# A streaming encoder step on one core: the relative bias copied to DRAM in eight parts, RWKV's low-rank weights loaded in the indexer, and RWKV's output transposed two chunks at a time

## The chip, the core and the metric

One core of a Trainium2 chip runs the whole program. The metric is the device time of one execution in microseconds; the lower, the better. The kernel before was run three times: 1328.97, 1330.21 and 1335.14 us, with a median of 1330.21 us.

## What is computed

One layer of a streaming encoder over 1024 prompt rows and 64 sample rows, with three mixers side by side and one output projection:

```
u = rms_norm(h)                       # 1088 rows x 1024
z = u @ w_in                          # all columns of all branches
A: RWKV-7: per head a 64x64 state, S = S * w + (S . -kk) (kk * a) + v k
   decay from tanh(w_in) @ w_b, rate from a_in @ a_b      (both of rank 64)
   y = group_norm(y) * lnx_w + lnx_b + (r.k.r_k) v
B: forgetting attention, causal, with a cumulated forget gate
C: sparse attention: indexer scores, top 256 keys per row, softmax with
   bias = t5_table[t5_bucket(key position - query position)]
h = h + concat(A * silu, B * silu, C * silu) @ w_out
y = rms_norm(h)
```

The change touches three things of this: how the bias of C comes to DRAM, when the two low-rank matrices `a_w_b` and `a_a_b` of A are loaded, and how the normalised `y` of A is turned to head-major form.

## The kernel before

**Stages.** The input rows are normalised and transposed to `uH` (rounded) and `uL` (the rest). Then the *indexer* projects the columns that the sparse branch's scores need and computes the scores of seven row tiles (`score[2]` to `score[7]` and `score["s"]`). Then *RWKV* works through 17 units of four 64-step chunks, while the top-k search runs beside it on VectorE and ScalarE. Then come the two attentions and the output projection.

**Projections as fill.** Every projection (`proj`, line 154) streams three matmuls per 128 columns of `u`: the weights' bf16 copy `wb` with `uL`, and the split weights `wh` and `wl` with `uH`. The weight tiles come in the order of `PLAN`, one 512 KB tile `wraw` after another (line 130, two buffers); ScalarE rounds it to `wh` (line 137), GpSimd makes `wl` and `wb` from it (lines 140 and 142). Projections of later branches are *fill*: `pump` puts pieces of them between the steps of indexer, RWKV and attention, so that TensorE has work while those wait. A projection writes one of two banks `pproj`; the bank is free when ScalarE and VectorE have read it (lines 802 to 806 in RWKV's inputs: `zs`, `zm`, `shift`).

**Order on the engines.** The program is written as generators that are braided by rates. On top of that, the framework's scheduler orders the instructions of each engine by a simulated timeline; so an instruction runs where its operands are ready by that simulation, and not where its line stands. Each engine works through its queue in order, and all transfers here are issued by SyncE, in order too. A transfer on SyncE that must wait holds up those behind it.

**The bias.** `relative_bias` (line 1242) multiplies the bias table with a one-hot matrix (`t5tab`, `t5oh`, into `t5ps`), copies the 8x384 result to `t5v` in SBUF, and writes it to DRAM 128 times over, as `d_t5` of 128x8x384 (line 1258; `d_t` in the profile). The sparse attention later reads from it a skewed view. The indexer drives this generator in three steps: at row tiles 3, 5 and "s".

**The low-rank weights.** `rwkv_pools` (line 1261) is called when the indexer is done. It loads the two 64x512 matrices twice each into a z tile `wabr` (line 1275), rounds them on ScalarE to `wabh` (line 1276) and leaves the rest in `wabl` on GpSimd (lines 1271 and 1278). `low_rank` (lines 1293 and 1294) multiplies them for every unit.

**The tail of a unit.** `tail` (line 1600) normalises `Yt`, 128 x 4 chunks x 64. Partitions hold two heads, columns a head's 64 values. Each chunk is transposed by itself to 64x128 in `ps_tp` (line 1625, by the helper at line 107), and two activations per span of chunks apply scale and bias (line 1631) from `lnx`, which has 64 partitions.

Of the kernel before, what the change touches and what calls it, by code (L numbers as in the profile page):

```python
# [12 lines left out]
F32 = mybir.dt.float32  # L13
F32R = mybir.dt.float32r
# [3 lines left out]
AF = mybir.ActivationFunctionType  # L18
OP = mybir.AluOpType
# [5 lines left out]
P = 128  # L25
# [60 lines left out]
class K:  # L86
# [183 lines left out]
    def setup(self):  # L270
        nc, I = self.nc, self.I
# [8 lines left out]

        self.trib = cp.tile([P, 2, 512], BF16, name="trib")
        nc.gpsimd.memset(self.trib, 0.0)
        self.lnx = cp.tile([64, 16], F32, name="lnx")
        self.par = cp.tile([P, 54], F32, name="par")
        self.omm = cp.tile([P, 13], F32, name="omm")
        self.par2 = cp.tile([P, 16], F32, name="par2")
# [1 line left out]
        with ExitStack() as c2:  # L288

            xa, xb = [self.xp.tile([P, D], F32, tag=f"x{i}", name="setup", bufs=1) for i in range(2)]  # L290
            rows = xb[:54, 0:P]
            con = xa[:, 0:C_M]
            nc.sync.dma_start(out=con, in_=I["consts"][:, 0:C_M])
            nc.vector.tensor_copy(self.con, con)
            nc.vector.tensor_scalar(self.trib[:, 1, 0:64], con[:, C_AM + 64:C_AM + 128], NEG, None, op0=OP.mult)
            tri = xb[:, P:2 * P]
            nc.sync.dma_start(out=tri, in_=I["consts"][:, C_TRI:C_ALL])
            nc.vector.tensor_copy(self.trib[:, 0, 384:512], tri)
            o = 0
            for nm, n in (("a_mu", 13), ("state_a_shift", 13), ("a_w0", 4), ("a_a0", 4), ("a_k_k", 4), ("a_k_a", 4), ("a_r_k", 4)):  # L300
                src = I[nm]
                names = " ".join(f"x{i}" for i in range(len(src.shape)))
                nc.sync.dma_start(out=rows[o:o + n, :], in_=src.rearrange(f"{names} -> ({names})").rearrange("(a p) -> a p", p=P))
                o += n
            self.PAR = dict(mu=0, sh=13, w0=26, a0=30, kk=34, ka=38, rk=42)
            lrows = xb[:16, 2 * P:2 * P + 64]
            nc.sync.dma_start(out=lrows[0:8, :], in_=I["a_lnx_w"].rearrange("x (a p) -> (x a) p", p=64))
            nc.sync.dma_start(out=lrows[8:16, :], in_=I["a_lnx_b"].rearrange("x (a p) -> (x a) p", p=64))
            ps = self.pt.tile([P, 4, P], F32, tag="xps", name="ps_setup").rearrange("p a b -> p (a b)")
            nc.tensor.transpose(ps[:, :46], rows[:46, :], self.ident[:46, :46])  # L310
            nc.tensor.transpose(ps[:64, 64:80], lrows, self.ident[:16, :16])
            nc.vector.tensor_copy(self.par[:, :46], ps[:, :46])
            nc.vector.tensor_scalar(self.lnx, ps[:64, 64:80], 0.5, None, op0=OP.mult)
        nc.vector.tensor_scalar(self.omm, self.par[:, 0:13], -1.0, 1.0, op0=OP.mult, op1=OP.add)

        nc.vector.tensor_scalar(self.par2[:, 0:4], self.par[:, 26:30], 0.5, None, op0=OP.mult)
# [81 lines left out]
    def indexer(self):  # L398
# [6 lines left out]
        with ExitStack() as c2:  # L405
# [54 lines left out]
            for i in list(range(2, 8)) + ["s"]:  # L460

                if i == 3:
                    gates = self.forget(ip, mrow)
                    next(gates)
                    bias = self.relative_bias(c2)
                    next(bias)
                if i == 4:
                    nc.sync.dma_start(out=O["p_c_kidx"][0, 0].rearrange("(a p) d -> p a d", p=P), in_=mrow[:, 0:8, 0:64])
                    nc.sync.dma_start(out=O["s_c_kidx"][0, 0], in_=mrow[:64, 8, 0:64])
                if i == 5:  # L470
                    next(bias)
                if i == 7:
                    next(gates, None)
                if i == "s":
                    next(bias, None)
                r = P if i != "s" else 64
                q0 = i * P - 256 if i != "s" else 768
                k0, kn = (0, (i + 1) * P) if i != "s" else (1024, 576)
# [763 lines left out]
    def relative_bias(self, ctx):  # L1242

        nc = self.nc
        self.d_t5 = self.dram.tile([P, 8, 384], F32, tag="d_t5", name="d_t5")
        p = self.pool("t5", ctx=ctx, right=True)
        pp = self.pool("t5p", space=PSUM, ctx=ctx, right=True)
        tb = p.tile([32, 8], F32, name="t5tab")
        oh = p.tile([32, 384], F32, name="t5oh")
        nc.sync.dma_start(out=tb, in_=self.I["t5_table"])  # L1250
        nc.sync.dma_start(out=oh, in_=self.I["onehot"])
        yield
        ps = pp.tile([P, 512], F32, name="t5ps")
        nc.tensor.matmul(ps[:8, :384], tb, oh, start=True, stop=True)
        vv = p.tile([8, 384], F32, name="t5v")
        nc.vector.tensor_copy(vv, ps[:8, :384])
        yield
        nc.sync.dma_start(out=self.d_t5.rearrange("q h r -> h q r"), in_=vv.rearrange("h (o r) -> h o r", o=1).broadcast_to([8, P, 384]))


    def rwkv_pools(self, c2):


        nc, I, O = self.nc, self.I, self.O
        one = self.pool("rw1", ctx=c2, right=True)
        self.gen = self.pool("gen", space=PSUM, ctx=c2)
        self.gring = lambda tag, bufs: (lambda dt=F32: self.gen.tile([P, 512], dt, tag=tag, name="ps_" + tag, bufs=bufs))

        self.wabh = one.tile([P, 2, 512], F32R, name="wabh")
        self.wabl = one.tile([P, 2, 512], F32R, name="wabl")  # L1270
        nc.gpsimd.memset(self.wabl.bitcast(F32), 0.0)
        raw = self.z("wabr")[:, 0:1024].rearrange("p (x c) -> p x c", x=2)
        for x, nm in enumerate(("a_w_b", "a_a_b")):
            for r in (slice(0, 64), slice(64, 128)):
                nc.sync.dma_start(out=raw[r, x], in_=I[nm][0])
        nc.scalar.copy(self.wabh, raw)
        for x, r in enumerate((slice(0, 64), slice(64, 128))):
            nc.gpsimd.tensor_tensor(self.wabl[r, x], raw[r, x], self.wabh[r, x], op=OP.subtract)
        self.one, self.state = one, None

        self.ND = [one.tile([P, 2, 4, P], F16, name=f"ND{i}") for i in range(2)]
        for t in self.ND:
            nc.gpsimd.memset(t, 0.0)
# [316 lines left out]
    def tail(self, one, x):  # L1600
# [20 lines left out]
        (g if PN & 2 else v).tensor_tensor(Yt, Yt, bc(st[:, 2]), op=OP.mult)  # L1621
        yield
        ps = self.tp()
        for c in range(4):
            self.turn(ps[0:64, c * P:c * P + P], Yt[:, c])
        q = ps[0:64].rearrange("p (c x t) -> p c x t", x=2, t=64)
        for hp, t0, o, n in x["spans"]:
            cs = slice(o // 64, (o + n) // 64)
            for h in range(2):
                hd = 2 * hp + h  # L1630
                sc.activation(yT[hv[h], cs], q[:, cs, 1 - h], AF.Identity, bias=self.lnx[:, 8 + hd:9 + hd], scale=self.lnx[:, hd:hd + 1])
        y = yT.rearrange("p c t -> p (c t)")
        g.tensor_tensor(y, y, x["vb"].rearrange("p c t -> p (c t)"), op=OP.add)
        g.tensor_tensor(y, y, gt, op=OP.mult)
# [121 lines left out]
def program(ctx, tc, I, O):  # L1756
# [24 lines left out]
    s.setup()  # L1781
    cx.close()
    with ExitStack() as c2:
        s.zs = s.pool("zs", bufs=1, ctx=c2, right=True)
        s.scp = s.pool("scp", ctx=c2, right=True)
        s.tkp = s.pool("tkp", ctx=c2, right=True)
# [19 lines left out]
        for u in range(n + 2):  # L1806
# [12 lines left out]
            if u < n:  # L1819
                work.append(("topk", topk, N_TOPK, (DVE, ACT)))  # L1820
            work = [w[:3] for w in work if w[0] != "topk"]
            s.free = u >= FE
            s.braid(work, R_T if u > n else R_END if len(work) < 3 and u else R_A / 10, ("topk", topk, N_TOPK, (DVE, ACT), work[-1][0] if SIDE < 0 else work[SIDE][0]) if u < n else None)
        for _ in topk:
# [89 lines left out]
```

## Time and profile before

| | |
|---|---|
| median of three runs | 1330.21 us |
| the profiled execution | 1331.56 us |
| its span | 1329.8 us |
| mean granted clock of TensorE | 0.979 |
| TensorE busy | 1258.4 us |
| VectorE, ScalarE, GpSimd busy | 847.5, 780.2, 669.7 us |
| moved by transfers | 168.78 MB, mean 127 GB/s |

In the profile PE is TensorE, PEld its weight loads, DVE VectorE, ACT ScalarE, POOL GpSimd and SP SyncE. An arrow `a<-b` reads: a written from b. What stands in brackets at the end of a row of the timeline is how long the engine stood before it, and what ended that. PEclk is the granted clock: 1.00 is 2.4 GHz, 0.50 is 1.2 GHz.

### The profile page before, as it was taken

How to read it: one execution, taken by the hardware profiler on the slowest of the kernel's cores; microseconds unless marked ns; L12 is line 12 of the kernel's file. 1: busy time of each engine (PE TensorE's matmuls, PEld its weight loads, DVE VectorE, ACT ScalarE, POOL GpSimd, SP SyncE). 2: the span in 40 equal slices, each digit the busy share in tenths (PEclk: the TensorE clock that was granted, in tenths of full speed). 3: DMA queues.
4: the chain of work that ended last, by engine and by line, in shares of the span. 5: the costliest groups of instructions: out<-in, count | busy, mean ns of one | idle time of the engine just before them, and what ended most of it. 6: DMA issues, size and time to landing. Idle time of an engine off the chain costs nothing.

```text
span 1329.8 us, 29357 instructions
## 1 busy us (share of the span) xinstructions
PE 1258.4 (95%) x10544; PEld 964.2 (73%) x10563; DVE 847.5 (64%) x2487; ACT 780.2 (59%) x1762; POOL 669.7 (50%) x973
## 2 busy tenths in 40 slices
PE   7969999999999999988999998999999989999997
PEld 5747676777777777766777677888988856777764
DVE  7338437887877777899754316556666479766642
ACT  7335427777777887644353346576665578655532
POOL 6223445445445456556464365566667567544311
PEclk9979999999999999988999998999999989999999
DMA  7352422222223324433232378867755576543323
GB/s 224 50 105 71 128 83 66 87 70 89 68 70 104 102 80 140 123 101 110 94 104 89 126 216 246 217 201 209 182 198 146 146 212 186 142 116 106 97 76 95
DMA packets 172460, 168.78 MB, mean 127 GB/s; under 512 B 38513, under 2 KB 147097, under 8 KB 172314
## 3 DMA queue, kind: packets, MB, share of 16 engines
q1 hardware_dynamic: 172314, 166.89, 43.9%
q8 instruction: 84, 1.38, 0.4%
q14 instruction: 62, 0.51, 0.1%
HBM read 104.61 MB, written 62.24 MB: 125 GB/s over the span
## 4 chain that ended last, share of the span: by engine, by line
PE 73%; DVE 11%; DMA 6%; ACT 3%; issue 3%; POOL 2%; SPq 1%; DVEq 0%; POOLq 0%; ACTq 0%
PE pproj L154 32%; PE pproj L1697 7%; PE ps_pv L993 5%; PE ps_atp L107 5%; PE ps_tp L1697 4%; PE ps_ga L1412 3%; DMA wraw<-in_w_in_dram 2%; PE ps_sc L962 2%; PE ps_sc L963 2%; PE ps_gb L1471 2%; PE ps_tp L107 1%; PE ps_gb L1478 1%; PE ps_gc L1581 1%; ACT junka L601 1%; PE ps_gc L1583 1%
## 5 line engine op out<-in xcount | busy, mean ns | idle before, releaser
L154 PE MATMUL pproj<-uH,wh 128*128 128x384 f32 (+4 forms) x1088 | 494.6, 455 | 0.0
L154 PE MATMUL pproj<-uH,wl 128*128 128x384 f32 (+4 forms) x1088 | 363.4, 334 | 0.0
L154 PE MATMUL pproj<-uL,wb 128*128 128x384 bf16 (+4 forms) x1088 | 359.4, 330 | 2.2 <-DVE shift L806 2.0
L154 PEld LDWEIGHTS pproj<-uH,wh 128*128 128x128 f32 (+1 forms) x1088 | 217.9, 200 | 3.9 <-issue 0.7
L154 PEld LDWEIGHTS pproj<-uH,wl 128*128 128x128 f32 (+1 forms) x1088 | 208.1, 191 | 2.2 <-issue 0.2
L154 PEld LDWEIGHTS <-wb 128*128 128x128 bf16 (+1 forms) x1088 | 106.6, 98 | 118.6 <-issue 81.5
L601 ACT ACTIVATE junka<-score,tk_tau 128x1024 f16<-128x1024 f32 (+4 forms) x160 | 149.4, 934 | 38.9 <-DVE junk L595 24.1
L914 POOL TENSOR_SCALAR S<-S,mx 128x128 f32<-128x128 f32 (+8 forms) x136 | 103.8, 766 | 83.7 <-DVE mx L913 60.4
L931 ACT CAST hl<-ps_atp 128x512 fp32r<-128x512 f32 (+3 forms) x184 | 93.4, 514 | 77.7 <-PE ps_atp L107 68.2
L140 POOL TENSOR_TENSOR wl<-wraw,wh 128x256 fp32r<-128x256 f32 (+1 forms) x184 | 137.1, 775 | 3.3 <-ACT wh L137 2.7
L932 DVE TENSOR_TENSOR hl<-ps_atp,hl 128x512 fp32r<-128x512 f32 (+3 forms) x184 | 109.7, 600 | 44.6 <-ACT hl L931 42.8
L142 POOL TENSOR_SCALAR wb<-wraw 128x512 bf16<-128x512 f32 (+1 forms) x92 | 60.3, 671 | 142.1 <-issue 60.7
L909 ACT ACTIVATE S<-S,mx 128x128 f32<-128x128 f32 (+8 forms) x136 | 105.8, 778 | 38.2 <-DVE mx L905 34.8
L993 PE MATMUL ps_pv<-hl,VS 128*128 128x256 f32 (+3 forms) x640 | 113.7, 290 | 7.7 <-ACT hl L931 3.2
L993 PEld LDWEIGHTS ps_pv<-hl,VS 128*128 128x128 f32 (+1 forms) x640 | 90.4, 176 | 20.8 <-DVE hl L932 5.0
L107 PE MATMUL ps_atp<-ident,S 128*128 128x128 f32 x616 | 103.6, 280 | 1.1 <-POOL S L914 0.8
L1159 POOL TENSOR_TENSOR cb<-nm,T 128x256 f32<-128x256 bf16 (+2 forms) x80 | 57.4, 724 | 52.7 <-DVE mx L905 51.1
L107 PEld LDWEIGHTS ps_atp<-ident,S 128*128 128x128 f32 x616 | 76.4, 144 | 7.7 <-issue 1.7
L137 ACT CAST wh<-wraw 128x1024 fp32r<-128x1024 f32 (+1 forms) x46 | 47.7, 1038 | 47.0 <-PE pproj L154 27.0
L1697 PE MATMUL pproj<-oh,gh 128*128 128x512 f32 x144 | 67.4, 490 | 0.6 <-ACT pproj L1745 0.3
L803 DVE SCALAR_TENSOR_TENSOR zm<-pproj,omm,zs 128x384 f32<-128x384 f32 (+2 forms) x52 | 25.8, 496 | 43.3 <-ACT zs L802 42.9
L1697 PE MATMUL pproj<-ol,gb 128*128 128x512 bf16 (+1 forms) x134 | 48.8, 386 | 1.4 <-DVE ol L1677 0.9
(383 smaller groups left out, 2849.6 us busy)
## 6 DMA issues: line engine op xcount, KB each, us to landing
wraw<-in_w_in_dram SPq DMA_DIRECT2D x45, 512.0 KB
oraw<-in_w_out_dram SPq DMA_DIRECT2D x12, 512.0 KB
out_dram<-rows SPq DMA_DIRECT2D x10, 512.0 KB
x<-in_x_prompt_dram SPq DMA_DIRECT2D x8, 512.0 KB
wt<-a_wa SPq DMA_DIRECT2D x16, 256.0 KB
b_v<-vs SPq DMA_DIRECT2D x8, 512.0 KB
VS<-b_v SPq DMA_DIRECT2D x8, 512.0 KB
d_y<-y SPq DMA_DIRECT2D x64, 64.0 KB
```

Of the source, the lines that this page charges most:

```text
L107: self.nc.tensor.transpose(out, x, self.ident[:n, :n])
L140: nc.gpsimd.tensor_tensor(l[:, k:k + 2, :n], raw[:, k:k + 2, :n], h[:, k:k + 2, :n], op=OP.subtract)
L142: nc.gpsimd.tensor_scalar(b[:, k:k + 4, :n], raw[:, k:k + 4, :n], 1.0, 0.0, op0=OP.mult, op1=OP.add)
L154: self.nc.tensor.matmul(ps[:n, :nt], a[:, k, :n], b[:, k, t0:t0 + nt], start=(k == 0 and i == 0), stop=(k == KD - 1 and i == 2))
L601: nc.scalar.activation(junk[:, :sc.shape[1]], sc, AF.Sign, bias=tf[:, j:j + 1], accum_out=cnt[:, j:j + 1])
L909: nc.scalar.activation(S[:, :kn], S[:, :kn], AF.Exp, bias=mx[:, nm - 1:nm], scale=-1.0, accum_out=mx[:, 6:7])
L914: nc.gpsimd.tensor_scalar(S[:, :kn], S[:, :kn], mx[:, 7:8], 0.5, op0=OP.mult, op1=OP.mult)
L931: nc.scalar.copy(ph[:kr, a:b], ps[:kr, a:b])
L932: nc.vector.tensor_tensor(pl[:kr, a:b], ps[:kr, a:b], ph[:kr, a:b], op=OP.subtract)
L993: nc.tensor.matmul(pv[0:m, q0:256], VS[:, kb, 0:m], hl[:, x, o:o + w], start=kb == 0 and x == 0, stop=at[-1][0] == last and n == 3)
L1159: nc.gpsimd.tensor_tensor(o, x, y, op=OP.add)
L1697: nc.tensor.matmul(ps[hf][:n, :], parts[m // 4][q][:, m % 4, :n], self.wo[m][q // 2][:, hf * 512:hf * 512 + 512], start=m == 0 and q == 0, ...
```

## The change

Three parts. The bias goes from `t5v` to one row `d_row` of 8x384 in DRAM, and from there in eight transfers of 16 copies each to `d_t5`; the generator yields between them, one step per RWKV unit from the second on. The loads and the splitting of the low-rank weights move into the indexer, at row tiles 3 and 5; the raw weights stay in the memory of `score[7]` until that tile's scores are written, and `wabh` and `wabl` have a pool of their own. In the tail, two chunks are transposed at once, 128x128, so that odd chunks come out on partitions 64 to 127; `lnx` gets a second copy on those partitions, and a span of several chunks takes four activations instead of two.

```diff
-        self.lnx = cp.tile([64, 16], F32, name="lnx")
+        self.lnx = cp.tile([P, 16], F32, name="lnx")
...
-            lrows = xb[:16, 2 * P:2 * P + 64]
-            nc.sync.dma_start(out=lrows[0:8, :], in_=I["a_lnx_w"].rearrange("x (a p) -> (x a) p", p=64))
-            nc.sync.dma_start(out=lrows[8:16, :], in_=I["a_lnx_b"].rearrange("x (a p) -> (x a) p", p=64))
+            lrows = xb[:16, 2 * P:3 * P]
+            for c in (slice(0, 64), slice(64, P)):
+                nc.sync.dma_start(out=lrows[0:8, c], in_=I["a_lnx_w"].rearrange("x (a p) -> (x a) p", p=64))
+                nc.sync.dma_start(out=lrows[8:16, c], in_=I["a_lnx_b"].rearrange("x (a p) -> (x a) p", p=64))
...
                 if i == 3:
...
-                    bias = self.relative_bias(c2)
-                    next(bias)
+                    self.bias = self.relative_bias(c2)
+                    next(self.bias)
+                    self.load_low_rank()
...
                 if i == 5:
-                    next(bias)
+                    next(self.bias)
+                    self.split_low_rank()
...
                 if i == "s":
-                    next(bias, None)
+                    next(self.bias)
...
         yield
-        nc.sync.dma_start(out=self.d_t5.rearrange("q h r -> h q r"), in_=vv.rearrange("h (o r) -> h o r", o=1).broadcast_to([8, P, 384]))
+        nc.sync.dma_start(out=row[:, :], in_=vv)
+        yield
+        for q in range(0, P, 16):
+            nc.sync.dma_start(out=self.d_t5[q:q + 16], in_=row.rearrange("(o h) r -> o h r", o=1).broadcast_to([16, 8, 384]))
+            yield
+
+    def load_low_rank(self):
+        nc, p = self.nc, self.lr
+        self.wabh = p.tile([P, 2, 512], F32R, name="wabh")
+        self.wabl = p.tile([P, 2, 512], F32R, name="wabl")
+        nc.gpsimd.memset(self.wabl.bitcast(F32), 0.0)
+        self.wabr = self.score[7].rearrange("p (x c) -> p x c", x=2)
+        for x, nm in enumerate(("a_w_b", "a_a_b")):
+            for r in (slice(0, 64), slice(64, 128)):
+                nc.sync.dma_start(out=self.wabr[r, x], in_=self.I[nm][0])
+
+    def split_low_rank(self):
+        nc = self.nc
+        nc.scalar.copy(self.wabh, self.wabr)
+        for x, r in enumerate((slice(0, 64), slice(64, 128))):
+            nc.gpsimd.tensor_tensor(self.wabl[r, x], self.wabr[r, x], self.wabh[r, x], op=OP.subtract)
...
-        for c in range(4):
-            self.turn(ps[0:64, c * P:c * P + P], Yt[:, c])
-        q = ps[0:64].rearrange("p (c x t) -> p c x t", x=2, t=64)
+        for j in range(2):
+            self.turn(ps[:, j * P:j * P + P], Yt[:, 2 * j:2 * j + 2].rearrange("p c t -> p (c t)"))
+        q = ps[:, :256].rearrange("p (j x t) -> p j x t", x=2, t=64)
         for hp, t0, o, n in x["spans"]:
-            cs = slice(o // 64, (o + n) // 64)
+            c0, c1 = o // 64, (o + n) // 64
             for h in range(2):
                 hd = 2 * hp + h
-                sc.activation(yT[hv[h], cs], q[:, cs, 1 - h], AF.Identity, bias=self.lnx[:, 8 + hd:9 + hd], scale=self.lnx[:, hd:hd + 1])
+                for i in range(2) if c1 - c0 > 1 else (c0 % 2,):
+                    sc.activation(yT[hv[h], (c0 + i if c1 - c0 > 1 else c0):c1:2], q[hv[i], c0 // 2:(c1 + 1) // 2, 1 - h], AF.Identity,
+                                  bias=self.lnx[hv[i], 8 + hd:9 + hd], scale=self.lnx[hv[i], hd:hd + 1])
...
+            if u:
+                next(s.bias, None)
             s.free = u >= FE
```

The six lines of `rwkv_pools` that loaded and split the low-rank weights are gone.

Since the scheduler decides the order, the places are shown as they come out. First SyncE's queue, near the end of the indexer's first projections. Before, `t5tab` and `t5oh` are the table and the one-hot matrix, `d_t_822` is the bias in DRAM and `wraw` a weight tile:

```order
L130 DMA wraw<-in_w_in_dram 128x8x128 x2
L1250 DMA t5tab<-in_t_table_dram 32x8
L1251 DMA t5oh<-in_onehot_dram 32x384
L1258 DMA d_t_822<-t5v 8x128x384
L130 DMA wraw<-in_w_in_dram 128x8x128 x2
L468 DMA out_dram<-mrow 128x8x64
```

And with the change, where `score_418` is the memory of `score[7]`:

```order
L130 DMA wraw<-in_w_in_dram 128x8x128 x2
L1254 DMA t5tab<-in_t_table_dram 32x8
L1255 DMA t5oh<-in_onehot_dram 32x384
L1278 DMA score_418<-in_a_w_b_dram 64x512 x2
L1278 DMA score_418<-in_a_a_b_dram 64x512 x2
L1262 DMA d_row<-t5v 8x384
L1265 DMA d_t_828<-d_row 16x3072 x8
L130 DMA wraw<-in_w_in_dram 128x8x128 x2
L470 DMA out_dram<-mrow 128x8x64
```

The four loads and the copy to `d_row` stand ahead of the bias copy; its eight parts stand together where the one transfer stood, between the same weight loads.

Second, TensorE where the first RWKV unit is prepared beside a projection. Before:

```order
L154 LDWEIGHTS wb
L154 MATMUL pproj<-uL,wb 128x320
L154 MATMUL pproj<-uH,wh 128x320
L154 MATMUL pproj<-uH,wl 128x320
L1293 MATMUL ps_ga<-wt,wabh 128x256
L1294 MATMUL ps_ga<-wt,wabl 128x256
L1331 MATMUL ps_ga<-ones,k_1709 128x2 x2
L154 LDWEIGHTS wb
```

And with the change:

```order
L154 MATMUL pproj<-uH,wl 128x384
L1307 MATMUL ps_ga<-wt,wabh 128x256
L1308 MATMUL ps_ga<-wt,wabl 128x256
L154 LDWEIGHTS wb
L154 MATMUL pproj<-uL,wb 128x320
L154 MATMUL pproj<-uH,wh 128x320
L154 MATMUL pproj<-uH,wl 128x320
```

The two low-rank matmuls stand four groups of 128x320 further ahead, right behind the last group of 128x384; the one with `ones` follows two groups later.

Third, GpSimd in the indexer, with the change; before, `wl` of line 140 is followed by `wb` of line 142 at once:

```order
L140 TENSOR_TENSOR wl<-wraw,wh 128x256 x4
L1274 MEMSET wabl 128x1024
L1284 TENSOR_TENSOR wabl<-score_418,wabh 64x512 x2
L142 TENSOR_SCALAR wb<-wraw 128x512 x2
L140 TENSOR_TENSOR wl<-wraw,wh 128x256 x4
```

The clearing and the two subtractions stand between two weight tiles, of which the second is the one whose `wb` starts at 53.64 us in the profile before. ScalarE's cast to `wabh` stands behind the second `KI` cast of the second key projection.

## Rows read from the trace of the kernel before

**Rows 1.** The page: busy time of the engines, and the chain by engine.

```profile
PE 1258.4 (95%) x10544; PEld 964.2 (73%) x10563; DVE 847.5 (64%) x2487; ACT 780.2 (59%) x1762; POOL 669.7 (50%) x973
...
PE 73%; DVE 11%; DMA 6%; ACT 3%; issue 3%; POOL 2%; SPq 1%; DVEq 0%; POOLq 0%; ACTq 0%
```

**Rows 2.** Timeline of TensorE, 74 to 90 us: start, duration, instruction.

```profile
74.89 0.34 PE L154 MATMUL pproj<-uL,wb 128*128 128x384 bf16 x1
...
75.42 0.34 PE L154 MATMUL pproj<-uL,wb 128*128 128x384 bf16 x1
...
75.77 0.34 PE L154 MATMUL pproj<-uH,wl 128*128 128x384 f32 x1
85.65 0.34 PE L453 MATMUL ps_tp<-ident,mT 76*64 76x76 f32 x1 [9.54 <-ACT mrow L454]
87.98 0.50 PE L154 MATMUL pproj<-uL,wb 128*128 128x384 bf16 x1 [2.00 <-DVE shift L806]
...
88.93 0.54 PE L154 MATMUL pproj<-uL,wb 128*128 128x384 bf16 x1
```

**Rows 3.** The chain that ended last, and ScalarE's timeline, between 57 and 85 us.

```profile
57.80 26.16 DMA wraw<-in_w_in_dram
...
84.06 1.04 ACT L137 CAST wh<-wraw 128x1024 fp32r<-128x1024 f32 x1 [15.09 <-DMA wraw<-in_w_in_dram]
```

**Rows 4.** The chain: a weight tile at 203.60 us, a 64 KB load at 1007.26 us.

```profile
203.60 4.20 DMA wraw<-in_w_in_dram
...
1007.26 2.23 DMA cQ<-c_q1h
```

**Rows 5.** Issues on SyncE between 40 and 50 us; size of the bias copy.

```profile
40.47 0.33 SPq L1251 DMA_DIRECT2D t5oh<-in_onehot_dram  x1
49.62 0.29 SPq L1258 DMA_DIRECT2D d_t<-t5v  x1
...
d_t<-t5v SPq DMA_DIRECT2D x1, 1536.0 KB
```

**Rows 6.** Windows: busy time by engine (PE, PEld, DVE, ACT, POOL), clock, DMA share, GB/s.

```profile
64.00:76.00 12.00, 12.00 (x75) 8.84 (x73) 1.24 (x2) 1.38 (x4) 0.00 (x0) 1.00 0.45 51
...
92.00:94.00 2.00, 2.00 (x11) 1.54 (x10) 0.54 (x3) 0.60 (x1) 2.00 (x4) 0.78 0.70 139
...
154.00:158.00 4.00, 4.00 (x25) 2.89 (x24) 1.59 (x4) 0.58 (x1) 4.00 (x6) 1.00 0.83 271
```

**Rows 7.** Where RWKV begins: timelines of TensorE and ScalarE, and one window.

```profile
164.32 0.38 PE L1293 MATMUL ps_ga<-wt,wabh 128*128 128x256 f32 x1 [2.12 <-ACT wabh L1276]
165.71 0.58 PE L1294 MATMUL ps_ga<-wt,wabl 128*128 128x256 f32 x1 [1.01 <-POOL wabl L1278]
...
158.06 0.51 ACT L1327 ACTIVATE k<-zt,par 128x256 f32<-128x256 f32 x1 [1.22 <-DMA zt<-a_k]
...
163.22 1.04 ACT L1276 CAST wabh<-wabr 128x1024 fp32r<-128x1024 f32 x1 [2.17 <-DMA wabr<-in_a_a_b_dram]
...
164.00:172.00 8.00, 6.68 (x26) 5.22 (x27) 1.77 (x4) 3.15 (x8) 5.98 (x8) 0.57 0.27 76
```

**Rows 8.** RWKV's stage, 160 to 800 us, as one window.

```profile
160.00:800.00 640.00, 612.58 (x6666) 460.18 (x6665) 432.57 (x1330) 392.46 (x912) 334.38 (x512) 0.98 0.34 103
```

**Rows 9.** Timeline of GpSimd, its first weight tile after the normalisation.

```profile
53.64 1.20 POOL L142 TENSOR_SCALAR wb<-wraw 128x512 bf16<-128x512 f32 x2 [21.27 <-PE pproj L154]
```

**Rows 10.** Timeline of TensorE: four transposes of either width, and one that follows.

```profile
262.93 0.60 PE L107 MATMUL ps_tp<-ident,Yt 128*64 128x128 f32 x4
263.46 0.33 PE L1564 MATMUL ps_gd<-za,UD 64*64 64x64 f32 x4
...
181.81 0.60 PE L107 MATMUL ps_ga<-ident,BK 128*128 128x128 f32 x4
```

**Rows 11.** ScalarE's groups by shape, line 1631: busy us, mean ns.

```profile
L1631 ACT ACTIVATE yT<-ps_tp,lnx 64x256 f32<-64x256 f32 x32 | 17.9, 558 | 5.3 <-PE ps_tp L107 4.8
L1631 ACT ACTIVATE yT<-ps_tp,lnx 64x64 f32<-64x64 f32 x8 | 3.2, 400 | 0.1
```

More of the change, by code (lines that the diff above doesn't have):

```diff
@@ L305, in setup @@
             self.PAR = dict(mu=0, sh=13, w0=26, a0=30, kk=34, ka=38, rk=42)
-            lrows = xb[:16, 2 * P:2 * P + 64]
-            nc.sync.dma_start(out=lrows[0:8, :], in_=I["a_lnx_w"].rearrange("x (a p) -> (x a) p", p=64))
-            nc.sync.dma_start(out=lrows[8:16, :], in_=I["a_lnx_b"].rearrange("x (a p) -> (x a) p", p=64))
+            lrows = xb[:16, 2 * P:3 * P]
+            for c in (slice(0, 64), slice(64, P)):
+                nc.sync.dma_start(out=lrows[0:8, c], in_=I["a_lnx_w"].rearrange("x (a p) -> (x a) p", p=64))
+                nc.sync.dma_start(out=lrows[8:16, c], in_=I["a_lnx_b"].rearrange("x (a p) -> (x a) p", p=64))
             ps = self.pt.tile([P, 4, P], F32, tag="xps", name="ps_setup").rearrange("p a b -> p (a b)")
             nc.tensor.transpose(ps[:, :46], rows[:46, :], self.ident[:46, :46])
-            nc.tensor.transpose(ps[:64, 64:80], lrows, self.ident[:16, :16])
+            nc.tensor.transpose(ps[:, 64:80], lrows, self.ident[:16, :16])
             nc.vector.tensor_copy(self.par[:, :46], ps[:, :46])
-            nc.vector.tensor_scalar(self.lnx, ps[:64, 64:80], 0.5, None, op0=OP.mult)
+            nc.vector.tensor_scalar(self.lnx, ps[:, 64:80], 0.5, None, op0=OP.mult)
         nc.vector.tensor_scalar(self.omm, self.par[:, 0:13], -1.0, 1.0, op0=OP.mult, op1=OP.add)
@@ L1244, in relative_bias @@
         nc = self.nc
+        row = self.dram.tile([8, 384], F32, tag="d_row", name="d_row")
         self.d_t5 = self.dram.tile([P, 8, 384], F32, tag="d_t5", name="d_t5")
@@ L1267, in rwkv_pools @@
         self.gring = lambda tag, bufs: (lambda dt=F32: self.gen.tile([P, 512], dt, tag=tag, name="ps_" + tag, bufs=bufs))
[L1269 to L1278, printed above, removed]
         self.one, self.state = one, None
@@ L1783, in program @@
     with ExitStack() as c2:
+        s.lr = s.pool("lr", ctx=c2, right=True)
         s.zs = s.pool("zs", bufs=1, ctx=c2, right=True)
```

## The prediction

> **What bounds the kernel now.** I read the page first: TensorE is busy for 95% of the span, and 73% of the chain that ended last is TensorE work [rows 1]. So the end moves by what TensorE gains or loses, and the 71 us in which it stands are the first thing to look for. In the page's 40 slices I looked for those where TensorE falls below nine tenths, and opened the timeline there. The largest stand runs from the end of the projection matmul of 75.77 us to 87.98 us with a single small transpose in between [rows 2]. The waits name the cause in steps. That transpose waits for ScalarE's copy of mrow; ScalarE, in order, stood in front of `wh` for a weight tile, 15.09 us until 84.06 us [rows 3]. The tile's transfer was issued at 57.80 us and landed 26.16 us later [rows 3], where an undisturbed one takes 4.20 us [rows 4]. What lay in its way is the copy of the relative bias `d_t`, one transfer of 1536 KB issued at 49.62 us [rows 5]: where it runs alone, 0.45 of the 16 DMA engines are busy and 51 GB/s move [rows 6]. 0.45 of 16 is 7 engines, and 1.573 MB at 51 GB/s is 30.8 us; with the weight loads that share those engines it fills the time to that landing.
>
> A second, smaller stand lies where the indexer ends and the first RWKV unit is prepared: TensorE waits 2.12 us for `wabh` and 1.01 us for `wabl`, which waited for the loads of the raw weights, and works at half clock until about 171 us [rows 7]. From there to 800 us TensorE stands for only 27.4 us of 640 [rows 8].
>
> **The bias copy.** The program spreads the eight parts over RWKV's units, but the order on SyncE, printed above, has all eight right behind `d_row`, ahead of the same two weight loads as before. So nothing is spread; what changes is the shape. The source is a 12 KB row in DRAM, the outer size is 16 instead of 8, and a short copy to `d_row` is added, for which SyncE waits. That wait is covered: between the issue at 49.62 us and that at 57.80 us SyncE has nothing else to issue [rows 3, 5]. In numbers: `t5v` is there at 49.6 us [rows 5]; `d_row` lands after some 2.2 us, by a 64 KB load's row [rows 4]; eight issues at 0.29 us, the issue of the old copy, take 2.3 us. The parts move from about 52 us. No row shows a DRAM-to-DRAM copy, so its rate is bounded. At the old pace of an engine, but on 16 of them, it is 51 / 0.45 = 113 GB/s and 13.9 us; at the 271 GB/s of the stretch in which RWKV's first stores and loads run at a share of 0.83 [rows 6], it is 5.8 us. They end at 58 to 66 us. I take the fast end, the row of traffic on all engines. The weight tile, issued at 57.80 us behind them, lands 4.20 us later, at 62 to 70 us.
>
> The Trainium skill, page "DMA: Bandwidth & Descriptors", section "Rules for kernel authors", says that an outermost size below 16 confines a transfer to at most so many engines; the 0.45 agrees with eight or fewer, and by this rule alone the new shape would run on all 16 and rival (a) below would be out. If the rule held and an engine kept its pace, the copy would take the 13.9 us of the slow bound and the sum would stay; if it did not hold, (a) gives the time.
>
> What is late next? Before, 4.0 us pass from the landing (83.96 us) to the free projection bank for which TensorE waits last (87.98 us) [rows 2, 3]. A tile that lands by 72 us is therefore early enough for TensorE at 76.1 us, and both bounds are. So the stand goes whole: 11.9 us less 0.2 for the transpose in it, 11.7. Behind it the granted clock stays at 0.5, the level of 1.2 GHz, until about 92.9 us [rows 6]; at 0.5 a group of three matmuls takes 0.95 us, at full clock 0.53, start to next start [rows 2], so of 4.9 us 2.2 go. **Term 1: -13.9 us.**
>
> **The low-rank weights.** On SyncE their four loads now follow the one-hot table's, whose issue is at 40.47 us, and SyncE's next issue before is at 49.62 us [rows 5]. GpSimd's clearing and subtractions lie in its 21.27 us of standing that end at 53.64 us [rows 9]. If the loads land 4.20 us after the last issue, as a tile does [rows 4], that is near 47 us; ScalarE's cast, 1.04 us [rows 7], would wait for them a microsecond or two and make the bias row late by as much. 2 us move the slow bound of the tile to 72 us and no further, so I cost it at 0; without that slack each microsecond would cost one. At the old place the wait for `wabh`, 2.12 us, and for `wabl`, 1.01 us, go. The clock's mean of 0.57 from 164 to 172 us [rows 7] makes 6.9 us at 0.5; 5.7 of them are work, which would take 3.1 by the groups above, so 2.6 go. The other inputs hold nothing up: `zt` was there for ScalarE at 158.06 us [rows 7], and the `a_wa` rows were issued just ahead of it; the two matmuls, moved up by four groups (`ones` by two), would run from about 160 us. **Term 2: -5.8 us.**
>
> **The turned output.** Per unit four transposes take 0.53 us of TensorE, start to next start, and the row of four is 0.60 long whether the stationary operand is 64 or 128 wide [rows 10]; two take 0.26. 17 units by 0.27 us: **term 3: -4.5 us**, as TensorE bounds that stretch. ScalarE pays: two activations of 64x256 at 558 ns become four of 64x128, between 400 and 558, say 455 [rows 11]: +0.7 us in 16 units, 11 us. ScalarE is busy for 392 of 640 us there, and all of TensorE's waits together are 27.4 us [rows 8]. Bounds are 0 and +11 us; I take 0, as 3% more of an engine with 39% free falls mostly into its own waits. The two further loads of `lnx` (0.29 us each on SyncE) precede weights that GpSimd takes up at 53.64 us only; 0.
>
> **The sum.** The profiled execution took 1331.56 us: -13.9 - 5.8 - 4.5 = -24.2 gives 1307.4. It stands 1.35 us over the median of the runs, 1330.21; against that, **1306 us**. The new sequence of ready times also changes the scheduler's order in all of RWKV's stage (some hundred rows on each engine change places). That I can't work out; I allow 10 us to either side, about a third of what TensorE stands there.
>
> **Rivals.** (a) *The copy is no faster.* All sixteen engines read one 12 KB row; if 51 GB/s is the pace of the source and not of seven engines, the parts run from 52 to 83 us and the tile, now behind them on every engine, lands at 87 us, 3 us later than before: +3 - 5.8 - 4.5 = -7.3, 1323 us. For it: no row shows such a read. Against it: 0.45 looks like a limit of engines.
> (b) *The copy is slower, and the kernel too.* The place is the same stand. The kernel is slower from where the tile lands later than 83.96 + 10.3 = 94.3 us, which is a copy of 38 us or 41 GB/s; by over 0.5% below 35 GB/s. At 25 GB/s, half the old pace, it lands at 119 us: +35 - 10.3, 1355 us. For it: source and destination share DRAM for the first time. Against it: 271 GB/s of stores to and loads from DRAM go side by side [rows 6].
> (c) *The new order gives it back.* RWKV's stage stands half as much again (+13.7: 1320 us) or twice (+27.4: 1333 us), most likely through ScalarE, whose top-k counts and the two further activations now meet differently. For it: VectorE's and ScalarE's rows change places throughout. Against it: term 1 lies before all of that, and the fill work that covers RWKV's waits is the same.
> (d) *Parts spread as written* would free the DMA engines even more, with the same term 1; it gives the same time.
>
> **How the numbers follow.** Forecast, with (d): 0.74, 1296 to 1316 us. (a): 0.09, about half on each side of 0.5%. (b): 0.06. (c): 0.11, half and half. A measurement of this kernel can tell about 0.5%, 6.7 us, from no change; so faster means below 1323.5 us: 0.74 + 0.05 + 0.06 = 0.85, the same 0.09, slower 0.06. The range is 1296 to 1321: the forecast's own, with the near part of (a) and (c).
>
> **What would show it.** Right: in the new profile the eight parts' window is under 15 us long with the DMA share near 1, the tile lands before 72 us, TensorE has no stand over 3 us between 50 and 100 us, the wait for `wabh` is gone, and the first RWKV matmul stands some 16 us earlier. Wrong: a tile that lands after 76 us ((a), (b)), or TensorE's idle time in RWKV's stage well above 27 us (c). If the stand at 76 us is gone and the end has not moved by 20 us, terms 2 and 3 or the new order failed, and the windows by stage tell which.

## The result, and the profile after

The change takes 1323.20 us, the median of 7 runs (1321.18 to 1325.77), against 1330.21 us before: a ratio of 0.9937 with a 95% interval of 0.992 to 0.9954. It is faster by some 7 us, just over the 0.5% that the prediction calls the least that can be told, where 24 were forecast; 1323.2 lies above the range of 1296 to 1321 us. The page after answers to [rows 1]; TensorE is as much the bound as before, and ScalarE is 10.9 us busier:

```profile
PE 1255.2 (95%) x10529; PEld 959.0 (73%) x10529; DVE 844.9 (64%) x2487; ACT 791.1 (60%) x1794; POOL 664.0 (50%) x973
...
PE 72%; DVE 9%; DMA 7%; ACT 4%; issue 3%; POOL 2%; SPq 2%; POOLq 0%; DVEq 0%; ACTq 0%
```

What the forecast said of the first 170 us is there. SyncE's timeline after (start, duration, instruction; answers to [rows 5]) has the short copy, the eight parts and the weight tile behind them:

```profile
48.63 0.29 SPq L1262 DMA_DIRECT2D d_row<-t5v  x1
50.00 4.96 SPq L1265 DMA_DIRECT2D d_t<-d_row  x8
56.79 0.40 SPq L130 DMA_DIRECT2D wraw<-in_w_in_dram  x1
```

Windows after, columns as in [rows 6]: while the parts run, the DMA engines are all busy (share 1.02) and move 289 GB/s. Where TensorE stood before [rows 2], it is busy without a gap, at full clock, and so it is where RWKV begins [rows 7]:

```profile
52.00:56.00 4.00, 4.00 (x23) 2.66 (x21) 1.14 (x2) 2.23 (x4) 3.28 (x5) 1.00 1.02 289
70.00:88.00 18.00, 18.00 (x106) 13.40 (x106) 15.00 (x40) 11.79 (x22) 10.06 (x13) 1.00 0.42 107
155.00:167.00 12.00, 12.00 (x80) 8.88 (x78) 4.65 (x14) 3.62 (x8) 4.66 (x10) 1.00 0.27 76
```

ScalarE's `wh` from the tile of 56.79 us runs at 70.87 us and waits for a projection there, no longer for the transfer:

```profile
70.87 1.05 ACT L137 CAST wh<-wraw 128x1024 fp32r<-128x1024 f32 x1 [2.89 <-PE pproj L154]
```

The loss lies behind. I cut both executions where TensorE first multiplies `QR` with `BK` (line 1412, now 1426) and at the first scores of the forgetting attention: the stages up to RWKV, RWKV, and the rest. Before:

```profile
0.00:186.91 186.91, 163.05 (x912) 120.75 (x912) 102.07 (x238) 86.25 (x171) 71.73 (x101) 0.95 0.44 112
186.91:791.78 604.87, 581.27 (x6486) 436.74 (x6485) 421.12 (x1293) 377.27 (x877) 316.19 (x483) 0.99 0.33 100
791.78:1329.80 538.02, 514.07 (x3148) 406.68 (x3167) 324.31 (x957) 316.67 (x715) 281.78 (x390) 0.98 0.58 163
```

After:

```profile
0.00:165.85 165.85, 157.13 (x910) 116.64 (x911) 102.22 (x237) 85.62 (x171) 72.74 (x101) 0.99 0.44 126
165.85:776.82 610.97, 580.79 (x6454) 435.63 (x6453) 419.56 (x1293) 391.22 (x910) 315.05 (x483) 0.98 0.33 99
776.82:1320.10 543.28, 517.29 (x3167) 406.69 (x3167) 323.10 (x957) 314.23 (x714) 276.18 (x390) 0.97 0.57 161
```

| stage | forecast | measured |
|---|---|---|
| up to RWKV | -13.9 - 5.8 = -19.7 | -21.1 |
| RWKV | -4.5 | +6.1 |
| the rest | 0 | +5.3 |
| span | -24.2 | -9.7 |

In RWKV's stage TensorE stands 611.0 - 580.8 = 30.2 us, before 23.6, and its busy time fell by only 0.5, at a granted clock of 0.98 instead of 0.99. Its longest waits there (what waited, for what: total, times, longest) end in VectorE's writes:

```profile
PE ps_gc L1586 <- DVE UV L1583: 4.6, 5, 2.7
PE ps_gb L1485 <- DVE Y L1523: 3.4, 6, 1.0
PE ps_gc L1595 <- DVE S L1591: 3.3, 6, 1.0
...
PE ps_gb L1485 <- DVE tk_need L659: 1.9, 1, 1.9
```

So did most of them before: summed by engine, VectorE ends 17.7 of the 21.6 us that this view lists for the stage before, and 22.3 of 28.8 after. The growth is spread over several of its writes.

### The profile page after: what moved, and what is told of

It is laid out like the page before. It is cut to its first block, busy times and chain, and to the rows that moved or that the text cites. A ratio compares the mean times of both kernels' runs of the same rounds, so it can differ in the third digit from the quotient of the medians.

```text
span 1320.1 us, 29357 instructions
## 1 busy us (share of the span) xinstructions
PE 1255.2 (95%) x10529; PEld 959.0 (73%) x10529; DVE 844.9 (64%) x2487; ACT 791.1 (60%) x1794; POOL 664.0 (50%) x973
## 4 chain that ended last, share of the span: by engine, by line
PE 72%; DVE 9%; DMA 7%; ACT 4%; issue 3%; POOL 2%; SPq 2%; POOLq 0%; DVEq 0%; ACTq 0%
PE pproj L154 34%; PE pproj L1714 6%; PE ps_pv L996 4%; PE ps_atp L107 4%; PE ps_tp L1714 3%; PE ps_ga L1426 2%; PE ps_sc L965 2%; PE ps_sc L966 2%; PE ps_gb L1485 2%; PE ps_gb L1492 1%; PE ps_gc L1595 1%; ACT junka L604 1%; DMA oraw<-in_w_out_dram 1%; PE ps_gc L1597 1%; PE ps_tp L107 1%
## 5 line engine op out<-in xcount | busy, mean ns | idle before, releaser
L140 POOL TENSOR_TENSOR wl<-wraw,wh 128x256 fp32r<-128x256 f32 (+1 forms) x184 | 134.2, 761 | 3.6 <-ACT wh L137 2.8
L1162 POOL TENSOR_TENSOR cb<-nm,T 128x256 f32<-128x256 bf16 (+2 forms) x80 | 50.5, 637 | 61.1 <-DVE mx L908 42.7
L1714 PE MATMUL pproj<-ol,gb 128*128 128x512 bf16 (+1 forms) x144 | 52.6, 391 | 0.2 <-DVE ol L1694 0.2
L1583 DVE COPY UV<-ps_gd 64x64 f32<-64x64 f32 x136 | 29.9, 220 | 34.9 <-PE ps_gd L1578 32.2
```

Of the source, the lines that this page charges most:

```text
L140: nc.gpsimd.tensor_tensor(l[:, k:k + 2, :n], raw[:, k:k + 2, :n], h[:, k:k + 2, :n], op=OP.subtract)
L1162: nc.gpsimd.tensor_tensor(o, x, y, op=OP.add)
L1714: nc.tensor.matmul(ps[hf][:n, :], parts[m // 4][q][:, m % 4, :n], self.wo[m][q // 2][:, hf * 512:hf * 512 + 512], start=m == 0 and q == 0, ...
```

## The experiments

Three theories. **S**: ScalarE's two further activations per unit make TensorE stand. **O**: the new order does, whatever the instructions. **L**: a lead is lost whatever one does, since later stages run into something fixed. The same cut of each kernel's own windows gives this table; "stands" is the stage less TensorE's busy time in it, from one trace per kernel, all in us. The ratio is to the kernel before on the same chip; since the experiments ran on several chips, kernels are best compared by it. e5 and e11 leave values out of the result. "Order" is explained at e9.

| kernel | RWKV starts | RWKV takes | stands | the rest | median | ratio (95%) |
|---|---|---|---|---|---|---|
| before | 186.9 | 604.9 | 23.6 | 538.0 | 1330.2 | 1 |
| the change | 165.9 | 611.0 | 30.2 | 543.3 | 1323.2 | 0.9937 (0.992-0.9954) |
| e1 bias copy alone | 172.6 | 607.4 | 23.1 | 538.6 | 1319.1 | 0.9906 (0.9881-0.9931) |
| e2 low rank alone | 181.3 | 608.6 | 21.9 | 539.6 | 1331.2 | 0.9998 (0.998-1.0016) |
| e3 tail alone | 189.1 | 608.4 | 30.2 | 537.4 | 1337.4 | 1.004 (1.0022-1.0057) |
| e4 no tail | 168.1 | 603.1 | 23.5 | 538.7 | 1313.4 | 0.987 (0.9845-0.9896) |
| e7 no tail, lnx | 167.7 | 603.2 | 24.0 | 540.4 | 1317.2 | 0.9889 (0.9866-0.9913) |
| e12 no tail, order 64 | 168.1 | 607.9 | 22.4 | 536.5 | 1315.6 | 0.9881 (0.9854-0.9909) |
| e6 four and four | 167.4 | 607.2 | 24.5 | 541.2 | 1318.1 | 0.9897 (0.9877-0.9916) |
| e16 the same, order 60 | 167.8 | 609.2 | 24.1 | 538.3 | 1309.1 | 0.9835 (0.981-0.986) |
| e17 the same, order 63 | 167.8 | 603.7 | 22.9 | 538.0 | 1314.5 | 0.9874 (0.9855-0.9893) |
| e5 two activations | 166.4 | 598.9 | 20.7 | 536.9 | 1304.4 | 0.9798 (0.9777-0.9819) |
| e11 the same, order 62 | 166.4 | 604.7 | 26.7 | 540.1 | 1313.2 | 0.9857 (0.9834-0.988) |
| e8 odd on VectorE | 167.8 | 599.7 | 20.7 | 541.7 | 1311.0 | 0.9842 (0.9819-0.9864) |
| e14 the same, order 63 | 166.5 | 600.6 | 21.0 | 538.0 | 1309.6 | 0.9832 (0.9807-0.9856) |
| e15 the same, order 60 | 166.9 | 604.5 | 25.3 | 538.2 | 1310.1 | 0.9839 (0.9814-0.9863) |
| e9 the change, order 60 | 167.2 | 612.6 | 27.2 | 539.2 | 1323.5 | 0.9931 (0.991-0.9953) |
| e10 the change, order 63 | 166.2 | 613.8 | 32.8 | 538.3 | 1317.8 | 0.9889 (0.9867-0.9911) |
| e18 the change, order 64 | 166.6 | 618.0 | 34.6 | 543.5 | 1329.4 | 0.9977 (0.996-0.9995) |
| e13 eight activations | 166.9 | 615.4 | 33.9 | 539.7 | 1324.9 | 0.9958 (0.9938-0.9977) |

### The parts one by one

e1 to e4 take hunks of the diff as they stand. In e1 the two calls for the low-rank weights are left out of the bias's hunks; e2 has these calls, their two functions and the pool; e3 has the tail's hunks and those of `lnx`; e4 is the change without e3's hunks.

e1, bias copy alone:

> The kernel before with the bias copy of the change alone; the order of every engine is that of before, but for the copy's own rows on SyncE. Theory O (the new order gives back): with the old order nothing is given back, so term 1 alone and in full: -13.9, about 1316 us, RWKV's TensorE idle 23 to 24 us as before. Theory L (a lead is given back, whatever the order, because the stages behind run into something that doesn't move): some 10 us are lost behind 175 us here too, 1325 us or more. Theory S (ScalarE's further activations in the tail give back): as O, 1316 us.

Measured: 0.9906, 12.5 us less, and the order of all other work is that of before. RWKV starts 14.3 us earlier, and 11.2 of them are left at the end of the trace, with 23.1 us of stands in RWKV's stage as before. So L falls: a lead is not lost by itself.

e2, low-rank weights alone:

> The kernel before with the low-rank weights moved alone; the scheduler reorders about as much as in the whole change. Theory O: term 2 (-5.8) is seen at the start of RWKV, and RWKV's and the attentions' stages differ from before by several us in either direction, so anywhere from 1320 to 1335 us, with the difference in stands and half clock behind 190 us. Theory L: about 1326 to 1330, the lead melts. Theory S: the full term 2, 1324 to 1325 us, and stages behind as before within 1 us.

Measured: RWKV starts 5.6 us earlier, as term 2 says, but the kernel is no faster. The stands are not what took it (21.9); TensorE is busy 586.7 us in RWKV's stage instead of 581.3 with the same instructions, at a clock of 0.98 instead of 0.99:

```profile
181.31:789.94 608.63, 586.70 (x6487) 440.31 (x6487) 420.79 (x1293) 378.57 (x878) 316.44 (x483) 0.98 0.33 99
```

S expected the full 5.8 and O anything; no gain is O's outcome, but the stands, by which O would take it back, are S's. Whether the order brings the lower clock or this one execution had it, one trace doesn't tell. Beside the bias copy the same part gave about what it should: from e1 to e4 the ratio falls from 0.9906 to 0.987, 4.8 us, though the two intervals overlap.

e3, tail alone:

> The kernel before with the two transposes and four activations of the tail alone (and the second copy of lnx); reordered too. Theory O: TensorE's work falls by 4 us, stands differ from before by several us in either direction: 1318 to 1335 us. Theory S: slower by 4 to 8 us, 1334 to 1338, with RWKV's TensorE waiting for ScalarE. Theory L: no lead, so term 3 holds: 1326 us.

Measured: slower by 0.4%, 5.3 us, inside S's 4 to 8. L's 1326 is out, and 1337.4 us lies 2 us above O's range. The stands are 30.2 us, the number of the whole change. But they are not the waits that S named: most of them end in VectorE's writes, few in ScalarE's (22.2 and 3.2 of the 26.9 us that the view lists).

e4, the change without its tail:

> The whole change without its tail: bias copy and low-rank weights, order of e2. Theory O: the time of e2 less 13.9 us. Theory S: terms 1 and 2 in full, -19.7, 1310 us. Theory L: as the whole change or slower, 1323 to 1327 us.

Measured: 1313.4 us, a ratio of 0.987: between S's 1310 and O's 1317, and L is out again. It is faster than the whole change by the 0.0067 between the ratios, 9 us, with 23.5 us of stands. The tail, forecast at -4.5 us, costs 9 beside the other two parts.

### What of the tail costs

e5 gives each span of several chunks two activations again (the even chunks' half, read twice):

```diff
-                for i in range(2) if c1 - c0 > 1 else (c0 % 2,):
-                    sc.activation(yT[hv[h], (c0 + i if c1 - c0 > 1 else c0):c1:2], q[hv[i], c0 // 2:(c1 + 1) // 2, 1 - h], AF.Identity,
...
+                    sc.activation(yT[hv[h], cs].rearrange("p (j i) t -> p j i t", i=2), q[hv[0], c0 // 2:c1 // 2, 1 - h].rearrange("p j (i t) -> p j i t", i=1).broadcast_to([64, m, 2, 64]), AF.Identity,
```

> The whole change, but a span of several chunks takes two activations of 64x256 again, as before: they read the even chunks' half of the turned tile twice, so the odd chunks' values are left out of the result. Two transposes stay, ScalarE's further 11 us go. Theory S (the two further activations of a unit make TensorE stand): RWKV's stage stands 23 to 24 us, as in e1, e2 and e4, and not 30 as in e3 and the whole change; e4's time less term 3, about 1309 us. Theory O (the tail's new order, whatever its activations): 30 us of stands or another number, time anywhere from 1309 to 1325. Theory W (it is the wide transposes that come late or hold TensorE): 30 us, about 1323.

Measured: 1304.4 us with 20.7 us of stands, both a little below what S said; W is out, and the time is below O's range too. RWKV's stage takes 12.1 us less than with four activations:

```profile
166.37:765.27 598.90, 578.20 (x6453) 433.38 (x6453) 417.28 (x1293) 379.74 (x878) 317.38 (x483) 0.99 0.33 101
```

e6 is the other half: e4 with `for i in range(2)` and every second chunk per activation, from four transposes:

> The change without its wide transposes: e4 with each span's two activations split into four of 64x128, from four transposes as before. ScalarE's further 11 us come alone. Theory S: RWKV's stands rise from 23.5 (e4) to about 30 us, with e4's time of 1313.4 plus 7 to 9, 1320 to 1322 us. Theory W: as e4, 1313 us. Theory O: stands between 22 and 32, 1311 to 1322 us, no rule.

Measured: 24.5 us of stands, as W said and not the 30 of S; 1318.1 us lies between the two, by the ratio 3.6 us above e4 and 1 above e7, within the intervals. O's wide range holds it as well. RWKV's window:

```profile
167.40:774.60 607.20, 582.72 (x6487) 438.20 (x6487) 420.10 (x1293) 386.11 (x910) 313.85 (x483) 0.99 0.33 100
```

ScalarE's timelines show the instructions, the two of before, e6's four and the change's four, each row one span:

```profile
263.57 1.13 ACT L1631 ACTIVATE yT<-ps_tp,lnx 64x256 f32<-64x256 f32 x2 [2.45 <-PE ps_tp L107]
```

```profile
243.04 1.61 ACT L1646 ACTIVATE yT<-ps_tp,lnx 64x128 f32<-64x128 f32 x4 [1.01 <-PE ps_tp L107]
```

```profile
241.27 1.86 ACT L1647 ACTIVATE yT<-ps_tp,lnx 64x128 f32<-64x128 f32 x4 [0.80 <-PE ps_tp L107]
```

e7 is e4 with the second copy of `lnx`, which nothing reads:

> e4 with the second copy of lnx alone: two further small loads at the start, nothing else added. The scheduler moves some hundred rows on each engine. It measures what a change of order without a change of work does. Theories S and W: as e4, 1312 to 1315 us, RWKV's stands 22 to 25 us. Theory O: stands move by 3 us or more, time by as much.

Measured: RWKV's stage as in e4 to 0.1 us, with 24.0 us of stands, as S and W said; the rest 1.7 us longer. The median of 1317.2 us is above their 1315, but by the ratio it is 2.5 us from e4, within the intervals. This small change of order was worth next to nothing in RWKV's stage.

e8 keeps the two wide transposes and gives the odd chunks to VectorE:

```diff
+                    elif ENG == "v" and i:
+                        v.tensor_scalar(dst, src, s_, b_, op0=OP.mult, op1=OP.add)
+                    else:
+                        sc.activation(dst, src, AF.Identity, bias=b_, scale=s_)
...
+ENG = "v"
```

> The whole change, with the odd chunks' scale and bias on VectorE, the even ones' on ScalarE. ScalarE is 3 to 4 us less busy than before, VectorE some 10 more. Theory S: the stands go back to about 24 us if it is ScalarE's time that counts, 1309 to 1313 us; if VectorE is as short of time, they stay at 30, 1320 us. Theory W: 1323 us. Theory O: between.

Measured: 1311.0 us, as S said for the case that it is ScalarE's time, with 20.7 us of stands where it said about 24; W is out. VectorE is 428.5 us busy in RWKV's stage, 9 more than in the change, and the stands don't show it:

```profile
167.80:767.50 599.70, 578.99 (x6454) 433.40 (x6453) 428.53 (x1329) 373.19 (x874) 314.45 (x483) 0.99 0.33 101
```

### Other orders of the same instructions

The scheduler's simulated timeline takes 61 cycles for a ScalarE read from PSUM. Set to another number, it gives another order of instructions that are otherwise the same:

```diff
+    _spec.ACCESS_CYCLES = {**_spec.ACCESS_CYCLES, (_b.MemoryType.PSUM, mybir.EngineType.Activation): 60}
```

e9 and e10, the whole change with 60 and 63:

> The whole change, every instruction the same; only the number of cycles that the scheduler's simulated timeline takes for a ScalarE read from PSUM is 60 instead of 61, so the order comes out anew. Theory S (ScalarE's two further activations make TensorE stand, in whatever order): RWKV's stage again stands near 30 us and takes 608 to 612 us, 1320 to 1326 us in all. Theory O (it was this order, and the activations only drew it): the stands fall anywhere between 20 and 30 us, and the time between 1304 and 1326, most likely under 1318.

> As e9 with 63 cycles: another order of the same instructions. Theory S: near 30 us of stands, 1320 to 1326 us. Theory O: not both of e9 and e10 near 30 us; at least one under 1318 us.

Measured: stands of 27.2 and 32.8 us, RWKV's stage 612.6 and 613.8. So the loss in RWKV is not this one order's. The times divide: e9's 1323.5 us is S's, e10's 1317.8 is below S's 1320 and just under O's 1318. The rest of the program, behind RWKV, takes 539.2 and 538.3 us instead of 543.3, with 21.3 and 22.1 us of stands instead of 26.0: so the change's 5.3 us there come with its own order or its one execution, not with its instructions; over all kernels of the table the rest takes 536.5 to 543.5 us.

e11 is e5 with 62, e12 is e4 with 64:

> As e5 (two activations, the odd chunks' values left out) with 62 cycles in the scheduler's timeline: another order of the same instructions. Theory S: as e5, 1302 to 1308 us, 19 to 23 us of stands. Theory O: 1304 to 1326, as likely above 1310 as below.

> As e4 (the change without its tail) with 64 cycles: another order of the same instructions. Theory S: as e4 and e7, 1312 to 1318 us, 22 to 25 us of stands. Theory O: 1306 to 1326 us, and a difference to e4 of 4 us or more either way.

Measured: e11 1313.2 us, above S's 1302 to 1308, with 26.7 us of stands; e12 1315.6 us with 22.4, as S said. Order alone moves RWKV's stage by up to 6 us (e5 to e11). In the stands the groups still don't overlap, if only by 0.5 us (26.7 against e9's 27.2).

### Load, and its company

e13 runs over `(0, 1, 0, 1)`, every activation twice; e14 and e15 are e8 with 63 and 60:

> The whole change with each span's four activations done twice; the result is the same, ScalarE is busy some 29 us more. So far RWKV's stage takes 599 to 605 us with two of them on ScalarE (e5, e8, e11) and 611 to 614 with four (the change, e9, e10), about one us for each us of ScalarE. Theory S: it grows on, to 625 to 645 us, and the time to 1336 to 1355 us. Theory O (the order, not ScalarE's load): 605 to 615 us again, 1315 to 1327 us.

> e8 with 63 cycles in the scheduler's timeline: another order of the same instructions. Theory S: RWKV's stage 598 to 605 us, 1308 to 1316 us. Theory O: 1304 to 1326 us, RWKV's stage as likely above 608 as below.

> e8 with 60 cycles in the scheduler's timeline, a third order. Theory S: RWKV's stage 598 to 605 us, 1308 to 1316 us. Theory O: 1304 to 1326 us, RWKV's stage as likely above 608 as below.

Measured: e13 is busy 419.1 us on ScalarE in RWKV's stage, 28 more than the change, and takes 615.4 us there, within the scatter of the change's own orders and at the edge of O's numbers. S's proportion, a us for a us, falls. e14 and e15 confirm e8 in other orders, inside S's ranges: 1309.6 and 1310.1 us.

e16 and e17 are e6 with 60 and 63, e18 the change with 64:

> e6 (four transposes, four activations) with 60 cycles in the scheduler's timeline: another order of the same instructions. Theory S in full (the price of the further activations doesn't depend on the transposes): RWKV's stage stands 28 us or more and takes 610 to 614 us, e6 was a lucky order. Theory P (the further activations are dear only behind the two wide transposes): 22 to 26 us of stands, 603 to 608 us, 1314 to 1319 us in all.

> As e16 with 63 cycles. Theory S in full: 28 us of stands or more, 610 to 614 us. Theory P: 22 to 26 us, 603 to 608 us.

> The whole change with 64 cycles, a fourth order of it. Theories S and P: RWKV's stands 27 to 33 us, its stage 610 to 615 us. Theory O: under 606 us.

Measured: behind four narrow transposes, four activations leave the stands at 24.5, 24.1 and 22.9 us, no more than two do (e4, e7, e12: 23.5, 24.0, 22.4). P's stands hold; e16's stage, 609.2 us, is above its 608, by busy time at a clock of 0.98, and its median, 1309.1 us, below its 1314. e18 is worse than any other order of the change; its stands and its stage lie above the 33 and 615 us that S and P allowed:

```profile
166.63:784.60 617.97, 583.32 (x6454) 436.86 (x6453) 417.89 (x1293) 392.32 (x910) 315.09 (x483) 0.98 0.32 98
```

Taken together, over all orders: the four orders of the change stand 27.2 to 34.6 us, 31.2 in the mean, and so do e3 and e13 (30.2, 33.9), which have its two wide transposes and four or more activations on ScalarE; the eleven others from e4 on stand 20.7 to 26.7, 23.3 in the mean, whether the transposes are narrow or two of the activations are gone or moved to VectorE; before, e1 and e2 stand 21.9 to 23.6. In the mean of ratios, the change's four orders have 0.9934, the three without the tail 0.988: the tail costs some 7 us. So the loss comes with the pair, two wide transposes and four activations on ScalarE, and with neither half alone, in every order tried.

The stands are not all of it. RWKV's stage takes 9.1 us more in the mean of the change's four orders than in the three without the tail: 7.9 of stands, and 1.2 of busy time, although the transposes save 4. The granted clock of the stage is 0.98 in all four, and 1.00, 1.00 and 0.98 without the tail. Time and clock go together in the runs of one kernel, too: of 23 runs of the kernel before, the five with a mean clock of 0.977 took 1332.9 to 1337.4 us, the four with 0.982 or more 1325.6 to 1329.7. What lowers the clock in the change is not shown.

Why the pair costs is open: a span's four take 0.25 us longer on ScalarE than e6's (1.86 against 1.61), and doubling them adds little, so length alone is not the reason. The pair also brings activations that read two halves of the partitions by turns, where e6's all read one; four that read one half twice running were not tried.

The best version that computes the whole result is e14, ratio 0.9832 (0.9807 to 0.9856): faster than both kernels, by 1% than the change, and the two other orders of the same kernel (e8, e15) agree within 0.001. e16 reaches 0.9835, but its other orders 0.9874 and 0.9897.

## Why the prediction was wrong, step by step

- **Term 1, -13.9 us: right.** The parts are issued from 50.00 to 54.96 us, the DMA share is 1.0 at 289 GB/s, the stand at 76 us is gone and the clock stays at 1.00. Alone it brought 12.5 us (e1). Of the two bounds the fast one held; rivals (a) and (b) are out. Two small steps were off and cancelled: an issue of a part takes 0.62 us, not 0.29, but the first comes 1.4 us behind `d_row`'s and not 2.2. The parts went all at once, as the order showed, so (d) was not tried.
- **The rule on the outermost size** (the Trainium skill, "DMA: Bandwidth & Descriptors", section "Rules for kernel authors") agrees: share 0.45 with 8, 1.02 with 16. But the source went from SBUF to DRAM and one transfer became eight at the same time, and no run parts the three. At 289 GB/s the copy did better than the 113 GB/s that sixteen engines at the old pace would give.
- **Term 2, -5.8 us: right at its place, uncertain at the end.** Its three pieces, 2.12, 1.01 and 2.6 us, add up to 5.7. Measured are 5.6 us at RWKV's start (e2) and 4.8 us in the ratio beside the bias copy, but nothing when alone, where RWKV's stage ran longer.
- **Term 3, -4.5 us: the saving is right, the step "ScalarE pays ... I take 0" failed.** The transposes of `Yt` are busy 6.8 us instead of 10.8, and the activations take 453 ns against the 455 assumed, +10.9 us on the page, as worked out. Their price for TensorE was put at 0, between bounds of 0 and +11. With two of the four on VectorE the tail is worth what term 3 said: mean ratio 0.9838 (e8, e14, e15) against 0.988 without it (e4, e7, e12), 5.6 us less. With all four on ScalarE it is 0.9934, 7 us more. So the term put at 0 measured some 13 us, a little over its far bound. In the change's own order the tail costs 9 us, alone 5.3 (e3). Of the 17 us that the forecast missed, this is the larger part, and most of the others are the 5.3 us behind RWKV. The reason given, that 39% of ScalarE was free, looked at the engine's mean; a mean does not tell when a result comes that others wait for in order. Yet behind narrow transposes the same two further activations cost nothing that can be told (e6, e16, e17: 0.9869 against 0.988), so the price is not ScalarE's time as such, and how it arises stays open.
- **"I allow 10 us to either side" for the new order** was the right size: four orders of the same change have medians from 1317.8 to 1329.4 us.
- **Rival (c)** came nearest: RWKV's stands grew from 23.6 to 30.2 us, with ScalarE's further activations in it as the text said, if by less than its 13.7 us. But it laid this to the new order, and all four orders of the change stand longer. A chance of 0.11 was too low, with a price known to be between 0 and 11 us against a saving of 4.5.

## What to carry to other kernels

Work that is taken from the bounding engine and given to another is not free just because that engine is 40% idle: where the engines work in order on each other's results, put the middle of its bounds into the sum, and try another engine for it, as VectorE here. Where a scheduler sets the order, an edit also draws a new one, and the same instructions scatter by 12 us in 1320: try the edit in three orders before a few us are credited to it. A table that is broadcast to DRAM can go faster as one short row and eight copies from it with an outer size of 16 than as one transfer from SBUF with an outer size of 8: here 289 GB/s against 51.

## What the runs showed of the hardware

- **A tiny VectorE operation can take 4 us beside GpSimd.** In VectorE's timeline of the change, a 128x8 conversion of the top-k search, 171 ns at the median of 31, takes 4.11 us, and `UV`, for which TensorE waits 2.7 us, comes behind it:

```profile
277.95 4.11 DVE L617 TENSOR_SCALAR tk_t<-tk_ge 128x8 int32<-128x8 f32 x1
282.10 0.64 DVE L618 TENSOR_TENSOR tk_tau<-tk_tau,tk_t 128x8 int32<-128x8 int32 x1
282.67 0.47 DVE L1583 COPY UV<-ps_gd 64x64 f32<-64x64 f32 x2
```

GpSimd's timeline shows no gap in that time:

```profile
277.79 0.40 POOL L1431 TENSOR_SCALAR ND<-BN 64x256 f16<-64x256 f32 x1 [2.97 <-DVE BN L1430]
278.16 1.20 POOL L142 TENSOR_SCALAR wb<-wraw 128x512 bf16<-128x512 f32 x2
279.33 0.66 POOL L1432 TENSOR_TENSOR ND<-BN,ND 64x256 f16<-64x256 f32 x1
279.96 2.76 POOL L140 TENSOR_TENSOR wl<-wraw,wh 128x256 fp32r<-128x256 f32 x4
```

The Trainium skill ("SBUF — State Buffer", section "Who interferes with whom") says that the two engines share a pair of ports, held for a whole instruction while the other is blocked, if VectorE works in a mode with two ports or reads two inputs from SBUF. A stand beside GpSimd agrees with that, but no trace shows VectorE's mode, and here it lasted over several of GpSimd's instructions, not one. It comes in e3, e9, e10 and e18 as well, beside the same run of GpSimd's instructions (4.11 to 4.12 us). But e6 and e17 have it with their low stands, and e13 stands 33.9 us without it, so it is not the reason for the loss.

- **An activation that goes over to other partitions starts later.** In the change each of a span's four activations of 64x128 reads the other half of the partitions than the one ahead of it, and they start 0.47 us apart, a little over the length of one (453 ns). In e6 all read partitions 0 to 63: the second of a head starts 0.36 us behind the first, before that one ends (447 ns), and the first of the next head, which writes other partitions, 0.46 us behind. So four take 1.86 us in the change and 1.61 in e6.
